# Cross-entropy of 256 rows on one core: the last partial sums in PSUM and added one by one, and new sizes for the loads

## The chip, the cores and the metric

The kernel runs on one core of a Trainium2 chip. The metric is the device time of one execution in microseconds; the median of several executions is compared.

## The reference

The inputs are logits (256 x 32000, fp32) and one label for each row. The result is one loss per row:

```python
log_probs = logits - np.max(logits, axis=-1, keepdims=True)
log_probs = log_probs - np.log(np.sum(np.exp(log_probs), axis=-1, keepdims=True))
return np.array([-log_probs[i, labels[i]] for i in range(batch)]).astype(np.float32)
```

That is the logarithm of the sum of exp(x) over a row, less the logit at the label. The kernel leaves out the maximum: it takes exp of the logits as they are, and multiplies the sum by exp(-logit at the label) before the logarithm.

## The kernel before, in words

The 256 rows are laid out as 128 partitions with two rows each, so a partition holds 64000 columns: row 0's 32000 and then row 1's. These columns are cut into 14 loads (`CHUNKS`), numbered 0 to 13, which SyncE's queue issues in order (`load`, L112). Loads 0 to 5 have buffers of their own. Load 6 takes over the buffer of load 2, and loads 7 to 13 lie side by side in `x_tail`, which takes over the buffer of load 1; so load 6 is issued once the exp of load 2 is done. The loads get smaller towards the end, so that little work is left when the last one lands.

ScalarE makes one pass over each load: `exps(i)` (L124) computes exp in place and sums along the columns into one accumulator, a column of `parts0` for row 0 or `parts1` for row 1. Load 3 holds the border between the two rows, so it is done in two pieces. On the chip each such call is two instructions, an ACTIVATE over the columns and an ACTIVATION_READ_ACCUMULATOR that writes the sum. The accumulator of the last load goes to a tile of its own, `s_last`.

Meanwhile GpSimd builds an identity matrix and gathers the logits at the labels (`g`); ScalarE takes exp(-g) (`eg`, L163), and VectorE multiplies the identity by it (`diag`, L165). A row is finished in this way: VectorE adds the columns of `parts` (`sums`), TensorE multiplies `sums` by `diag`, which gives the 128 scaled sums side by side on one partition of PSUM (`lane`), and ScalarE takes the logarithm (`log_row`, L132). Row 0 is finished in the middle of the stream (L169, L170). Row 1 is finished at the end: the reduction L177 waits for the accumulators up to load 12, L178 opens an accumulation in `lane1`, L180 adds `s_last` to it, then come the logarithm and the store of the result (L182).

After the exp of load 8 (`WARM_FROM`), TensorE is given 12 matmuls into a tile `warm` whose result nobody reads (L176). Every fp32 matmul is two instructions on TensorE, and each has a weight load.

The order on every engine is the order in which the program is written (`tc.manual_schedule()`); each engine works its queue from the front, and waits there for what its next instruction needs.

Of the kernel before, what the change touches and what calls it, by code (L numbers as in the profile page):

```python
# [9 lines left out]
P = 128  # L10
ROWS = 2
F32 = mybir.dt.float32
# [3 lines left out]


CHUNKS = [
    1024, 15104, 12672, 8960, 7136, 4992, 3872,
    2848, 2144, 1600, 1216, 992, 800, 640,  # L20
]
SLOTS = [0, 1, 2, 3, 4, 5, 2]
TAIL = len(SLOTS)
# [1 line left out]

WARM_FROM = 8
WARM = 12


def begin_first_load_before_barrier(nc):  # L30
# [15 lines left out]
@with_exitstack  # L46
def kernel(
    ctx: ExitStack,
    tc: tile.TileContext,
    logits: bass.AP,  # L50
    labels: bass.AP,
    out: bass.AP,
):
    nc = tc.nc
    nc.at_finalize(begin_first_load_before_barrier)
    B, C = logits.shape
    assert B == P * ROWS and sum(CHUNKS) == ROWS * C


    flat = logits.rearrange("(p r) c -> p (r c)", r=ROWS)  # L60


    pieces = []
    starts = []
    at = 0
    for n in CHUNKS:
        starts.append(at)
        cuts = [at] + [c for c in range(C, ROWS * C, C) if at < c < at + n] + [at + n]
        pieces.append([(a, b, a // C) for a, b in zip(cuts, cuts[1:])])
        at += n  # L70
    last = len(CHUNKS) - 1

    turn = next(i for i in range(len(CHUNKS)) if starts[i] + CHUNKS[i] >= C)

    big = ctx.enter_context(tc.tile_pool(name="big", bufs=1))
    small = ctx.enter_context(tc.tile_pool(name="small", bufs=1))
    psum = ctx.enter_context(tc.tile_pool(name="psum", bufs=1, space=bass.MemoryType.PSUM))

    width = {}
    for i, s in enumerate(SLOTS):  # L80
        width[s] = max(width.get(s, 0), CHUNKS[i])
    tiles = []
    for i, s in enumerate(SLOTS):
        tiles.append((big.tile([P, width[s]], F32, name=f"x{i}", tag=f"slot{s}"), starts[i]))
    tail = big.tile([P, width[TAIL_SLOT]], F32, name="x_tail", tag=f"slot{TAIL_SLOT}")
    assert sum(CHUNKS[TAIL:]) <= width[TAIL_SLOT]
    tiles += [(tail, starts[TAIL])] * (len(CHUNKS) - TAIL)

    n_of = [sum(1 for ps in pieces[:-1] for q in ps if q[2] == r) for r in range(ROWS)]
    parts = [small.tile([P, n_of[r]], F32, name=f"parts{r}") for r in range(ROWS)]  # L90
    s_last = small.tile([P, 1], F32, name="s_last")
    res = small.tile([1, ROWS * P], F32, name="res")
    sums = small.tile([P, ROWS], F32, name="sums")
    ident = small.tile([P, P], F32, name="ident")
    diag = [small.tile([P, P], F32, name=f"diag{r}") for r in range(ROWS)]
    lane = [psum.tile([1, P], F32, name=f"lane{r}") for r in range(ROWS)]
    warm = psum.tile([1, P], F32, name="warm")
    lbl = small.tile([P, 2 * ROWS], I32, name="lbl")
    idx = small.tile([P, ROWS], I32, name="idx")
    g = small.tile([P, ROWS], F32, name="g")  # L100
    eg = small.tile([P, ROWS], F32, name="eg")

    nc.scalar.preload_act_table_set("natural_log_exp_and_others")  # L103

    lbl_words = dataclasses.replace(
        labels.tensor, shape=[labels.tensor.shape[0] * 2], dtype=I32
    )

    def load(i):
        t, base = tiles[i]  # L110
        a, b = starts[i], starts[i] + CHUNKS[i]
        nc.sync.dma_start(out=t[:, a - base:b - base], in_=flat[:, a:b])  # L112

    seen = [0] * ROWS

    def exps(i):
        t, base = tiles[i]
        for a, b, r in pieces[i]:
            if i == last:
                acc = s_last[:, :]  # L120
            else:
                acc = parts[r][:, seen[r]:seen[r] + 1]
                seen[r] += 1
            nc.scalar.activation(  # L124
                out=t[:, a - base:b - base],
                in_=t[:, a - base:b - base],
                func=AF.Exp,
                accum_out=acc,
            )

    def log_row(r):
        nc.scalar.activation(  # L132
            out=res[0:1, r:ROWS * P:ROWS], in_=lane[r][:, :], func=AF.Ln
        )

    with tc.manual_schedule():
        first = len(set(SLOTS))
        for i in range(first):
            load(i)

        nc.scalar.dma_start(
            out=lbl[:, :], in_=bass.AP(tensor=lbl_words, offset=0, ap=[[2 * ROWS, P], [1, 2 * ROWS]])
        )
        nc.gpsimd.iota(out=idx[:, :], pattern=[[C, ROWS]], base=0, channel_multiplier=ROWS * C)
        make_identity(nc, ident[:, :])
        nc.gpsimd.tensor_add(out=idx[:, :], in0=idx[:, :], in1=lbl[:, 0:2 * ROWS:2])  # L146
        for r in range(ROWS):
            nc.gpsimd.indirect_dma_start(  # L148
                out=g[:, r:r + 1],
                out_offset=None,  # L150
                in_=logits[:, :],
                in_offset=bass.IndirectOffsetOnAxis(ap=idx[:, r:r + 1], axis=1),
            )


        done = 0
        for i in range(first, len(CHUNKS)):
            slot = SLOTS[i] if i < TAIL else TAIL_SLOT
            while done <= SLOTS[:first].index(slot):
                exps(done)  # L160
                done += 1
            load(i)
        nc.scalar.activation(out=eg[:, :], in_=g[:, :], func=AF.Exp, scale=-1.0)  # L163
        for r in range(ROWS):
            nc.vector.tensor_scalar_mul(diag[r][:, :], ident[:, :], eg[:, r:r + 1])  # L165
        for i in range(done, last):
            exps(i)
            if i == turn:
                nc.vector.reduce_sum(out=sums[:, 0:1], in_=parts[0][:, :], axis=mybir.AxisListType.X)  # L169
                nc.tensor.matmul(lane[0][:, :], sums[:, 0:1], diag[0][:, :], start=True, stop=True)  # L170
            if i == turn + 1:
                log_row(0)
            if i == WARM_FROM:
                col = parts[1][:, seen[1] - 1:seen[1]]
                for _ in range(WARM):
                    nc.tensor.matmul(warm[:, :], col, diag[0][:, :], start=True, stop=True)  # L176
        nc.vector.reduce_sum(out=sums[:, 1:2], in_=parts[1][:, :], axis=mybir.AxisListType.X)  # L177
        nc.tensor.matmul(lane[1][:, :], sums[:, 1:2], diag[1][:, :], start=True, stop=False)  # L178
        exps(last)
        nc.tensor.matmul(lane[1][:, :], s_last[:, :], diag[1][:, :], start=False, stop=True)  # L180
        log_row(1)
        nc.sync.dma_start(  # L182
            out=out.rearrange("(a n) -> a n", a=2), in_=res[0:1, :].rearrange("o (a n) -> o a n", a=2)
        )
# [30 lines left out]
```

The softmax here doesn't subtract the row's maximum and nothing guards it: scores larger than these inputs give would overflow.

## Time and profile before

| | |
|---|---|
| median of 5 runs | 84.49 us (84.3 to 86.21) |
| profiled execution, time | 85.67 us |
| profiled execution, span | 83.9 us |
| busy in the span: ScalarE | 58.4 us (70%) |
| busy: TensorE, matmul | 6.5 us (8%) |
| busy: VectorE | 0.8 us (1%) |
| logits read | 32.77 MB, mean 391 GB/s |
| DMA on the chain that ended last | 44% of the span |
| ScalarE on the chain that ended last | 32% of the span |

The slices of the page divide the span into 40 parts of 2.1 us, and a digit gives the busy tenths of a part. The chain of waits goes back from the last instruction to what released it at each step. In the timeline a line gives the start, the length, the engine and line, the operation, what it writes and reads, and in brackets the idle time ahead of it with what ended it. PE is TensorE's matmul, PEld its weight loads, ACT is ScalarE, DVE is VectorE.

### The profile page before, as it was taken

To read this page: it belongs to the slowest core of one execution; us is meant where nothing else is said; L and a number is where in the kernel's file an instruction comes from. 1 tells how busy PE (TensorE), PEld (TensorE's weight loads), DVE (VectorE), ACT (ScalarE), POOL (GpSimd) and SP (SyncE) were. 2 spreads that over 40 slices of the span, in tenths; PEclk is the share of its full clock that TensorE was granted. 3 is DMA by queue.
4 is the path that set the end of the run, shared out by engine and by line. 5 is a ranking of instruction groups with operands and counts; after the bars stand their busy time and mean duration, and the time that the engine had idled before them with its cause. 6 is when DMAs were issued, how large, how long until landed. Compare 5 with 4: busy or idle time off the path is not lost.

```text
span 83.9 us, 174 instructions
## 1 busy us (share of the span) xinstructions
PE 6.5 (8%) x30; PEld 3.4 (4%) x30; DVE 0.8 (1%) x4; ACT 58.4 (70%) x34; POOL 3.0 (4%) x10
## 2 busy tenths in 40 slices
PE   0000000000000000000000002000000000009980
PEld 0000000000000000000000000000000000005540
DVE  0000000000000000000000020000000000000000
ACT  6320000000299999909999999998999999999960
POOL 3000000000072000000000000000000000000000
PEclk9999999999999999999999999999999999999999
DMA  4999999998999989899997999999989999999200
GB/s 113 598 432 461 461 461 432 403 432 362 435 435 435 387 387 411 387 496 461 393 479 342 439 422 436 436 427 438 430 379 451 420 413 421 412 412 408 82 0 0
DMA packets 2226, 32.77 MB, mean 391 GB/s; under 512 B 433, under 2 KB 434, under 8 KB 1202
## 3 DMA queue, kind: packets, MB, share of 16 engines
q1 hardware_dynamic: 2018, 32.77, 92.0%
q10 hardware_dynamic: 144, 0.00, 0.1%
q0 software_dynamic: 64, 0.00, 0.1%
HBM read 32.77 MB, written 0.00 MB: 391 GB/s over the span
## 4 chain that ended last, share of the span: by engine, by line
DMA 44%; ACT 32%; issue 13%; PE 7%; SPq 0%; another core or an unknown queue 0%
DMA x<-in_logits_dram 44%; ACT x L124 26%; PE warm L176 6%; ACT x_tail L124 5%; ACT res L132 1%; PE lane L178 1%; SPq L112 0%; PE lane L180 0%; ACT eg L163 0%
## 5 line engine op out<-in xcount | busy, mean ns | idle before, releaser
L124 ACT ACTIVATE x<-x 128x1024 f32<-128x1024 f32 (+7 forms) x8 | 46.4, 5794 | 22.0 <-DMA x<-in_logits_dram 22.0
L124 ACT ACTIVATE x_tail<-x_tail 128x2848 f32<-128x2848 f32 (+6 forms) x7 | 9.8, 1404 | 0.0
L176 PE MATMUL warm<-diag,parts 128*1 128x128 f32 x24 | 5.3, 416 | 23.2 <-ACT x_tail L124 23.2
L170 PE MATMUL lane<-diag,sums 128*1 128x128 f32 x2 | 0.6, 397 | 51.8 <-DVE sums L169 51.8
L176 PEld LDWEIGHTS warm<-diag,parts 128*1 128x1 f32 x24 | 2.9, 122 | 25.6 <-ACT x_tail L124 23.7
L170 PEld LDWEIGHTS lane<-diag,sums 128*1 128x1 f32 x2 | 0.1, 80 | 51.8 <-DVE sums L169 51.8
L148 POOL DMA_INDIRECT g<-in_logits_dram,idx x2 | 2.1, 1040 | 0.6 <-issue 0.3
L103 ACT ACT_TABLE_LOAD x1 | 1.3, 1283 | 0.8 <-PEq L199 0.8
L124 ACT ACTIVATION_READ_ACCUMULATOR x<-x 128x1 f32 x8 | 1.5, 186 | 0.0
L124 ACT ACTIVATION_READ_ACCUMULATOR x_tail<-x_tail 128x1 f32 x7 | 1.3, 185 | 0.0
L132 ACT ACTIVATE res<-lane 1x128 f32<-1x128 f32 x2 | 0.5, 265 | 0.7 <-PE lane L180 0.7
L146 POOL TENSOR_TENSOR idx<-idx,lbl 128x2 int32<-128x2 int32 x1 | 0.2, 197 | 21.3 <-DMA lbl<-in_labels_dram 21.3
L165 DVE TENSOR_SCALAR diag<-ident,eg 128x128 f32<-128x128 f32 x2 | 0.5, 284 | 48.9 <-ACT eg L163 48.9
L178 PE MATMUL lane<-diag,sums 128*1 128x128 f32 x2 | 0.6, 418 | 0.0
L180 PE MATMUL lane<-diag,s_last 128*1 128x128 f32 x2 | 0.4, 302 | 0.0
L177 DVE TENSOR_REDUCE sums<-parts 128x1 f32<-128x10 f32 x1 | 0.2, 164 | 28.4 <-ACT x_tail L124 28.4
masks.py:199 POOL TENSOR_SCALAR_AFFINE_SELECT ident<-ident 128x128 f32<-128x128 f32 x1 | 0.3, 294 | 0.1
L178 PEld LDWEIGHTS lane<-diag,sums 128*1 128x1 f32 x2 | 0.3, 126 | 0.2
L180 PEld LDWEIGHTS lane<-diag,s_last 128*1 128x1 f32 x2 | 0.2, 122 | 0.2
masks.py:197 POOL MEMSET ident<- 128x128 f32 x1 | 0.2, 194 | 0.0
L163 ACT ACTIVATE eg<-g 128x2 f32<-128x2 f32 x1 | 0.2, 187 | 0.0
L169 DVE TENSOR_REDUCE sums<-parts 128x1 f32<-128x4 f32 x1 | 0.2, 157 | 2.3 <-ACT x L124 2.3
(5 smaller groups left out, 0.6 us busy)
## 6 DMA issues: line engine op xcount, KB each, us to landing
x<-in_logits_dram SPq DMA_DIRECT2D x1, 7552.0 KB, 21.8
x<-in_logits_dram SPq DMA_DIRECT2D x1, 6336.0 KB, 36.6
x<-in_logits_dram SPq DMA_DIRECT2D x1, 4480.0 KB, 46.7
x<-in_logits_dram SPq DMA_DIRECT2D x1, 3568.0 KB, 54.7
x<-in_logits_dram SPq DMA_DIRECT2D x1, 2496.0 KB, 60.0
x<-in_logits_dram SPq DMA_DIRECT2D x1, 1936.0 KB
x_tail<-in_logits_dram SPq DMA_DIRECT2D x1, 1424.0 KB, 21.6
x_tail<-in_logits_dram SPq DMA_DIRECT2D x1, 1072.0 KB, 23.7
```

Of the source, the lines that this page charges most:

```text
L103: nc.scalar.preload_act_table_set("natural_log_exp_and_others")
L124: nc.scalar.activation(out=t[:, a - base:b - base], in_=t[:, a - base:b - base], func=AF.Exp, accum_out=acc,)
L132: nc.scalar.activation(out=res[0:1, r:ROWS * P:ROWS], in_=lane[r][:, :], func=AF.Ln)
L146: nc.gpsimd.tensor_add(out=idx[:, :], in0=idx[:, :], in1=lbl[:, 0:2 * ROWS:2])
L148: nc.gpsimd.indirect_dma_start(out=g[:, r:r + 1], out_offset=None, in_=logits[:, :], in_offset=bass.IndirectOffsetOnAxis(ap=idx[:, r:r + 1 ...
L163: nc.scalar.activation(out=eg[:, :], in_=g[:, :], func=AF.Exp, scale=-1.0)
L165: nc.vector.tensor_scalar_mul(diag[r][:, :], ident[:, :], eg[:, r:r + 1])
L169: nc.vector.reduce_sum(out=sums[:, 0:1], in_=parts[0][:, :], axis=mybir.AxisListType.X)
L170: nc.tensor.matmul(lane[0][:, :], sums[:, 0:1], diag[0][:, :], start=True, stop=True)
L176: nc.tensor.matmul(warm[:, :], col, diag[0][:, :], start=True, stop=True)
L178: nc.tensor.matmul(lane[1][:, :], sums[:, 1:2], diag[1][:, :], start=True, stop=False)
L180: nc.tensor.matmul(lane[1][:, :], s_last[:, :], diag[1][:, :], start=False, stop=True)
```

## The change

The sizes of the 14 loads are new; their number, their order and their sum stay. Load 1 grows from 15104 to 16384 columns, and most of the last ones shrink.

The accumulators of loads 7 to 12 no longer go to columns of `parts1`. Each has a PSUM tile of its own (`far`). After the exp of such a load, VectorE copies the tile to SBUF (`near`), and TensorE multiplies it by `diag1` and adds it to `lane1`. The reduction of `parts1` and the matmul that opens the accumulation in `lane1` move from the end to just after the exp of load 6. At the end only `s_last` is left to be added. Both lanes now lie in one PSUM tile. The 12 warm matmuls stay behind load 8, now also behind the addition of load 8, and read a column of the exp's output instead of the accumulator.

So TensorE's queue from load 6 on is: the opening matmul, additions 7 and 8, the 12 warm matmuls, additions 9 to 12, and `s_last`. Before it was: the 12 warm matmuls, the opening matmul, and `s_last`.

```diff
 CHUNKS = [
-    1024, 15104, 12672, 8960, 7136, 4992, 3872,
-    2848, 2144, 1600, 1216, 992, 800, 640,
+    1024, 16384, 12512, 9024, 6656, 5088, 3744,
+    2688, 2016, 1504, 1120, 864, 736, 640,
 ]
...
+IN_PSUM = range(7, 13)
...
+    far = {i: psum.tile([P, 1], F32, name=f"far{i}") for i in IN_PSUM}
+    near = {i: small.tile([P, 1], F32, name=f"near{i}") for i in IN_PSUM}
...
-    lane = [psum.tile([1, P], F32, name=f"lane{r}") for r in range(ROWS)]
+    lane_tile = psum.tile([1, ROWS * P], F32, name="lane")
+    lane = [lane_tile[:, r * P:(r + 1) * P] for r in range(ROWS)]
...
+            elif i in IN_PSUM:
+                acc = far[i][:, :]
...
+            if i == IN_PSUM[0] - 1:
+                nc.vector.reduce_sum(out=sums[:, 1:2], in_=parts[1][:, :], axis=mybir.AxisListType.X)
+                nc.tensor.matmul(lane[1][:, :], sums[:, 1:2], diag[1][:, :], start=True, stop=False)
+            if i in IN_PSUM:
+                nc.vector.tensor_copy(out=near[i][:, :], in_=far[i][:, :])
+                nc.tensor.matmul(lane[1][:, :], near[i][:, :], diag[1][:, :], start=False, stop=False)
             if i == WARM_FROM:
-                col = parts[1][:, seen[1] - 1:seen[1]]
+                at = starts[i] - tiles[i][1]
+                col = tiles[i][0][:, at:at + 1]
                 for _ in range(WARM):
                     nc.tensor.matmul(warm[:, :], col, diag[0][:, :], start=True, stop=True)
-        nc.vector.reduce_sum(out=sums[:, 1:2], in_=parts[1][:, :], axis=mybir.AxisListType.X)
-        nc.tensor.matmul(lane[1][:, :], sums[:, 1:2], diag[1][:, :], start=True, stop=False)
         exps(last)
         nc.tensor.matmul(lane[1][:, :], s_last[:, :], diag[1][:, :], start=False, stop=True)
         log_row(1)
```

More of the change, by code (lines that the diff above doesn't have):

```diff
@@ L87 @@
     tiles += [(tail, starts[TAIL])] * (len(CHUNKS) - TAIL)
-    n_of = [sum(1 for ps in pieces[:-1] for q in ps if q[2] == r) for r in range(ROWS)]
+    n_of = [
+        sum(1 for ps in pieces[:IN_PSUM[0]] for q in ps if q[2] == r) for r in range(ROWS)
+    ]
+    assert all(len(pieces[i]) == 1 for i in IN_PSUM) and turn < IN_PSUM[0]
+    far = {i: psum.tile([P, 1], F32, name=f"far{i}") for i in IN_PSUM}
+    near = {i: small.tile([P, 1], F32, name=f"near{i}") for i in IN_PSUM}
     parts = [small.tile([P, n_of[r]], F32, name=f"parts{r}") for r in range(ROWS)]
```

## The prediction

> **What bounds the kernel now.** I read the slices of the page first, then the chain of waits, then the last ten microseconds instruction by instruction.
>
> ```profile
> PE   0000000000000000000000002000000000009980
> ACT  6320000000299999909999999998999999999960
> DMA  4999999998999989899997999999989999999200
> ```
>
> The DMA row is full up to slice 37; ScalarE (ACT) is full from slice 12, with dips where it waits for a load. The logits come in at a fixed pace and the exps follow them closely. PE works only in the last four slices, almost without a gap.
>
> ```profile
> 75.55 0.04 issue
> 75.59 5.28 PE warm L176 x24
> 80.87 0.43 PE lane L178 x2
> 81.30 0.25 PE lane L180 x2
> 81.54 0.02 issue
> 81.57 0.27 ACT res L132
> ```
>
> These are the last pieces of the chain of waits: start, length, what. The end already comes through TensorE's queue: 24 warm passes (each fp32 matmul is two instructions, a pass each), L178's two, L180's two, then the logarithm. The timeline of the same stretch shows how little room TensorE has:
>
> ```profile
> 75.35 0.18 ACT L124 ACTIVATION_READ_ACCUMULATOR x_tail<-x_tail 128x1 f32 x1
> ...
> 75.59 5.28 PE L176 MATMUL warm<-diag,parts 128*1 128x128 f32 x24 [23.16 <-ACT x_tail L124]
> ...
> 79.93 0.18 ACT L124 ACTIVATION_READ_ACCUMULATOR x_tail<-x_tail 128x1 f32 x1
> 80.03 0.72 ACT L124 ACTIVATE x_tail<-x_tail 128x640 f32<-128x640 f32 x1
> 80.15 0.16 DVE L177 TENSOR_REDUCE sums<-parts 128x1 f32<-128x10 f32 x1 [28.36 <-ACT x_tail L124]
> 80.45 0.34 PEld L178 LDWEIGHTS lane<-diag,sums 128*1 128x1 f32 x2
> 80.65 0.18 ACT L124 ACTIVATION_READ_ACCUMULATOR x_tail<-x_tail 128x1 f32 x1
> 80.66 0.63 PE L178 MATMUL lane<-diag,sums 128*1 128x128 f32 x2
> 80.89 0.33 PEld L180 LDWEIGHTS lane<-diag,s_last 128*1 128x1 f32 x2
> 81.09 0.44 PE L180 MATMUL lane<-diag,s_last 128*1 128x128 f32 x2
> 81.57 0.27 ACT L132 ACTIVATE res<-lane 1x128 f32<-1x128 f32 x1 [0.73 <-PE lane L180]
> ```
>
> The warm passes start when load 8's accumulator is read and run for 5.28 us; ScalarE's remaining work from there also takes 5.3 us (75.45 to 80.74). The two meet at the end by a hair: s_last was ready at 80.83, its weights loaded at 80.89, and its first pass started at 81.09, 0.21 behind L178's second (80.88). TensorE is a second limit of equal height beside ScalarE. That decides what follows.
>
> How long is one pass? From the first warm pass (75.59) to L178's first (80.66) lie 24 passes: 0.211 us each. The answers for L176 and L180 add their durations:
>
> ```profile
> L176 PE MATMUL warm<-diag,parts x24: 371/418/418, 75.6 to 80.5; 128*1 128x128 f32 x24
> ```
>
> ```profile
> L180 PE MATMUL lane<-diag,s_last x2: 273/302/331, 81.1 to 81.3; 128*1 128x128 f32 x2
> ```
>
> The same shape takes 418 ns up to 80.9, 331 at 81.09 and 273 at 81.26: TensorE got faster only at about 81.1, some 5.5 us after the chain of passes began, although the page's PEclk prints 9 in every slice. So the warm passes run slow, and only the very last ones fast. The length of a fast pass is bounded by these rows: if of the 418 ns only the 211 of the pitch shrinks, 273 leaves 0.066 us; if all shrinks alike, 0.211 x 273/418 = 0.138. I take the middle, 0.105.
>
> **The change, part by part.** The profiled execution took 85.67 us for a span of 83.9, so 1.77 lies outside. It is 1.18 above the median of the runs, 84.49; I work out a difference on this execution and carry it to the median.
>
> *Sizes.* The total is the same, so the last load lands when it did: by the trace's completions at 79.68. Between completions I interpolate by columns (1.19 ns per column from load 1 on, nearly straight). The new loads 1 to 6 land at 24.1, 39.1, 49.8, 57.7, 63.7 and 68.1 (before: 22.6, 37.8, 48.4, 56.8, 62.7, 67.3). An exp costs 0.833 ns per column ((2558 - 719) / (2848 - 640)) and 0.19 per piece (load 8's 2144 columns: 73.47 to 75.45). Walking ScalarE along these, it ends at 80.73 for the old sizes (the trace: 80.74) and 80.68 for the new. The later arrival of load 1 is hidden by a smaller stall before load 2 (1.1 for 2.3). Sizes alone: -0.05. They also move the end of load 8's exp, which releases TensorE: the loads 0 to 8 hold 384 columns more, and it ends 0.2 to 0.3 later.
>
> *Accumulators in PSUM.* From one READ_ACCUMULATOR to the next exp pass 0.10 us (75.35 to 75.45). No row writes one to PSUM. The nearest with a PSUM operand is L132: 63.00 to the next exp at 63.16, less 128 x 0.833 ns, leaves 0.05, where eg, two columns from SBUF, leaves 0.09 (48.56 to 48.65). I take 0.04 less for each of six, -0.25 in all, because that row has the same engine and the memory in question; the ends are 0 (the saving belongs to reading only) and -0.09 x 6 = -0.55, with +0.25 as its mirror. The walk then ends at 80.43, -0.30, load 8's accumulator at 75.62 (before 75.44), and ScalarE starts each of the last seven loads within 0.1 of its landing where it now is 0.2 to 0.35 behind.
>
> [...]
>
> *Copies on VectorE.* Six copies of 128x1, each waiting for one accumulator. VectorE is otherwise idle here, so they cost nothing to ScalarE; what they cost is on TensorE's path. Start about 0.11 after the accumulator, as L177 did (80.03 to 80.15); length between L177's 0.16 and L165's 0.28, I take 0.2; 0.05 to TensorE (L169 to L170). The addition of load 8 thus reaches TensorE at about 76.0. Row 1's early sum (L184, L185 of the new file) and the addition of load 7 run in gaps before that and cost nothing; if they were late they would only push this start.
>
> *Additions on TensorE.* This is where the price lies. The queue runs in order: addition 8 (2 passes), warm (24), additions 9 to 12 (8), s_last (2). Twelve warm matmuls still stand in front of four additions whose data come at 77 to 80, and in front of s_last. From 75.59 there were 28 passes; now there are 36 from 76.0, as addition 8 with its detour over VectorE stands ahead of the warm ones too, which only wait for ScalarE. L178 no longer comes behind them, which is in that count.
>
> With the slow pass throughout, the last of 36 starts at 76.0 + 35 x 0.211 = 83.4 and ends at 83.8, against 81.53: +2.3. If TensorE turns fast as long after the chain's start as before (5.5: at 81.5), 26 passes are begun by then, the 36th starts at 82.4 and ends, with 273 ns, at 82.7: +1.2. If it turns fast at the same moment as before (81.1), 24 are begun, and it ends at 82.5: +1.0. If it turned 2 us sooner than before, at 79.1, 15 are begun, the 36th starts at 81.3 and ends at 81.5: no difference. All of this is later than ScalarE needs (s_last at about 80.6, end then near 81.2), so the 0.30 gained there is not seen.
>
> [...]
>
> Of +1.0 and +1.2 I take +1.0, the unchanged moment, because a little more work (row 1's sum, addition 7) now precedes the chain. For the profiled execution that is 86.7, for the median 84.49 + 1.0 = 85.5.
>
> **Rivals.**
>
> 1. *ScalarE sets the end* (faster). TensorE would have to make its 35 steps by 80.9, within 4.9 us of 76.0; with 0.211 and 0.105 that means at most 12 slow ones, so fast passes from 78.5 on, 2.6 us sooner than in the trace. Then the whole -0.30 comes through, 84.2; from 79.1 back, a part of it. For it: the trace holds only one such turn, and does not show what sets its moment. Against: that one came after 5.5 us of unbroken passes, and here it would need half.
>
> 2. *No difference.* The turn comes close to 79.1, and the overhang of TensorE eats just what ScalarE gains: 84.3 to 84.7. It needs two sizes to meet.
>
> 3. *Slow to the end.* Fast passes are seen for two instructions only, and nothing in the trace says that they must come by 83.4. Without them +2.0 to +2.3, some 86.6.
>
> 4. *The change doesn't do what it says:* a saved accumulator read of 0. Then load 8 ends at 75.70 instead of 75.62, and the forecast moves by +0.1 only, since TensorE ends last; it is in the forecast's range.
>
> **How the numbers follow.** Forecast (TensorE ends last, turning fast within 1.5 us of 81.1 either way, which by the same count gives +0.2 to +1.7): 0.68. Slow to the end: 0.13. ScalarE sets the end: 0.13. No difference: 0.06. The range, 84.5 to 86.5, takes the forecast with its unknown moment and most of the slow case, and leaves out the faster one and the slowest runs, together under 0.2. About 0.2% (0.17 us) is what a measurement of this kernel can tell from no change. Faster 0.13, same 0.06, slower 0.81.
>
> **What would show it.** Right: in the profile after, the last exp ends up to 0.3 earlier against the last landing, the passes of additions 9 to 12 follow the warm ones without a gap although their copies were done before, and the idle time of the last L132 before "PE lane" grows from 0.73 to about 2. READ_ACCUMULATOR of a PSUM tile to the next exp takes 0.06 rather than 0.10. Wrong: if TensorE idles ahead of s_last, or its passes are near 0.105 apart before 79, rival 1 holds; if ScalarE stalls in the tail, the sizes were mis-walked.

## The result, and the profile after

The changed kernel is slower, by about half of what was forecast. Over 52 runs of it and 94 of the kernel before, the ratio is 1.0054 (95% interval 1.0031 to 1.0076), about +0.46 us; the medians of all runs are 85.82 and 85.21 us. On one chip side by side (the run `a_again` below) it is 1.0069 (1.0031 to 1.0107), +0.58 us, and the medians of all runs are 85.39 and 84.44. A ratio leaves out every run over 1.5% above the fastest of its kernel, here 27 of the 52 and 35 of the 94, whatever made them long, so executions in which TensorE turned fast late may be among them and +0.46 may be too small. The forecast was +1.0, that is 85.5, with a range of 84.5 to 86.5.

The profiled execution took 84.67 us for a span of 82.9. These are the last pieces of its chain of waits (start, length, what):

```profile
74.90 0.17 DVE near L187
75.07 0.04 issue
75.11 0.59 PE lane L188 x2
75.70 3.73 PE warm L193 x24
79.43 0.87 PE lane L188 x8
80.31 0.23 PE lane L195 x2
80.54 0.02 issue
80.56 0.27 ACT res L142
```

From addition 8 to the logarithm, the chain is TensorE alone: addition 8, the warm passes, additions 9 to 12 (x8), s_last. ScalarE's tail, five exps long, is not on it. The timeline of the same stretch tells when each part was ready:

```profile
74.71 0.16 ACT L134 ACTIVATION_READ_ACCUMULATOR x_tail<-x_tail 128x1 f32 x1
74.76 1.45 ACT L134 ACTIVATE x_tail<-x_tail 128x1504 f32<-128x1504 f32 x1
74.90 0.16 DVE L187 COPY near<-far 128x1 f32<-128x1 f32 x1 [1.67 <-ACT x_tail L134]
...
75.11 0.59 PE L188 MATMUL lane<-diag,near 128*1 128x128 f32 x2 [1.25 <-DVE near L187]
...
76.31 0.16 DVE L187 COPY near<-far 128x1 f32<-128x1 f32 x1 [1.25 <-ACT x_tail L134]
...
79.27 1.04 PE L188 MATMUL lane<-diag,near 128*1 128x128 f32 x8
79.48 0.23 ACT L134 ACTIVATION_READ_ACCUMULATOR x_tail<-x_tail 128x1 f32 x1
80.04 0.19 PEld L195 LDWEIGHTS lane<-diag,s_last 128*1 128x1 f32 x2
80.14 0.38 PE L195 MATMUL lane<-diag,s_last 128*1 128x128 f32 x2
80.56 0.27 ACT L142 ACTIVATE res<-lane 1x128 f32<-1x128 f32 x1 [0.85 <-PE lane L195]
```

Load 9's copy was done at 76.47, and its addition waited until 79.27 behind the warm matmuls. s_last was ready at 79.71 and its first pass began at 80.14. The accumulator now costs 0.05 us to the next exp (74.71 to 74.76), where it was 0.10. And the warm passes are not what they were in the first profile of before:

```profile
L193 PE MATMUL warm<-diag,x_tail x24: 272/276/417, 75.5 to 79.2; 128*1 128x128 f32 x24
```

Their median is 276 ns where it was 418: TensorE turned fast at 77.85, in the middle of the warm matmuls and 2.7 us after addition 8 began, not 5 after it. So this execution lost little: its logarithm starts only 0.85 after the last accumulator.

### The profile page after: what moved, and what is told of

Read it like the earlier page. It is cut to its first block, busy times and chain, and to the rows that moved or that the text cites. A ratio compares the mean times of both kernels' runs of the same rounds, so it can differ in the third digit from the quotient of the medians.

```text
span 82.9 us, 204 instructions
## 1 busy us (share of the span) xinstructions
PE 7.2 (9%) x42; PEld 3.7 (4%) x42; DVE 1.7 (2%) x10; ACT 58.2 (70%) x34; POOL 3.0 (4%) x10
## 4 chain that ended last, share of the span: by engine, by line
DMA 45%; ACT 32%; issue 13%; PE 7%; SPq 0%; DVE 0%
DMA x<-in_logits_dram 45%; ACT x L134 26%; ACT x_tail L134 5%; PE warm L193 5%; PE lane L188 2%; ACT res L142 1%; SPq L120 0%; PE lane L195 0%; DVE near L187 0%; ACT eg L173 0%
## 5 line engine op out<-in xcount | busy, mean ns | idle before, releaser
L134 ACT ACTIVATE x<-x 128x1024 f32<-128x1024 f32 (+7 forms) x8 | 46.9, 5866 | 21.0 <-DMA x<-in_logits_dram 21.0
L134 ACT ACTIVATE x_tail<-x_tail 128x2688 f32<-128x2688 f32 (+6 forms) x7 | 9.1, 1346 | 0.0
L193 PE MATMUL warm<-diag,x_tail 128*1 128x128 f32 x24 | 3.9, 338 | 0.0
L193 PEld LDWEIGHTS warm<-diag,x_tail 128*1 128x1 f32 x24 | 2.5, 105 | 1.4
L188 PE MATMUL lane<-diag,near 128*1 128x128 f32 x12 | 2.2, 313 | 3.1 <-DVE near L187 3.1
L187 DVE COPY near<-far 128x1 f32<-128x1 f32 x6 | 0.9, 158 | 7.4 <-ACT x_tail L134 7.4
L188 PEld LDWEIGHTS lane<-diag,near 128*1 128x1 f32 x12 | 0.8, 83 | 4.3 <-DVE near L187 4.1
L195 PE MATMUL lane<-diag,s_last 128*1 128x128 f32 x2 | 0.4, 272 | 0.0
```

Source lines behind the costliest of these rows:

```text
L134: nc.scalar.activation(out=t[:, a - base:b - base], in_=t[:, a - base:b - base], func=AF.Exp, accum_out=acc,)
L187: nc.vector.tensor_copy(out=near[i][:, :], in_=far[i][:, :])
L188: nc.tensor.matmul(lane[1][:, :], near[i][:, :], diag[1][:, :], start=False, stop=False)
```

## The experiments

Two theories and a third stood against each other. Queue: TensorE is still busy with the warm matmuls and four additions when s_last is ready. Sizes (or their landings): ScalarE or the DMA queues lose. Clock: the last passes are slow, wherever they stand. For each kernel the table gives the ratio to before on the same chip (for the changed one's first profile, over all its runs), and, from its profile, two stretches of the end: from the last landing (by the trace's completions) to the end of the last accumulator, which is ScalarE's part, and from there to the start of the last logarithm, which is TensorE's. The last column, the turn, is how long after the start of unbroken passes TensorE turned fast, by the clock's record in the trace, or by the lengths of the passes where it has none.

| kernel | ratio (95%) | ScalarE's part | TensorE's part | turn |
|---|---|---|---|---|
| before, first profile | | 1.16 | 0.73 | 5.6 |
| b_again | | 1.10 | 0.47 | 3.8 |
| changed, first profile | 1.0054 (1.0031 to 1.0076) | 0.98 | 0.85 | 2.7 |
| a_again | 1.0069 (1.0031 to 1.0107) | 0.97 | 1.77 | 4.6 |
| e1_sizes_only | 1.0035 (1.0004 to 1.0065) | 1.20 | 0.47 | 3.7 |
| e2_old_sizes | 1.0103 (1.0068 to 1.0138) | 0.89 | 1.48 | 4.7 |
| e3_warm0 | 1.0004 (0.9979 to 1.0028) | 0.98 | 0.68 | none |
| e3_warm6 | 0.9987 (0.9959 to 1.0016) | 0.98 | 0.72 | none before the end |
| e3_warm18 | 1.0304 (1.0264 to 1.0343) | 0.98 | 2.30 | 3.0 |
| e6_same12_moved | 0.9978 (0.9955 to 1.0002) | 0.99 | 0.47 | 2.7 |
| e2_old_sizes_warm6 | 0.9980 (0.9955 to 1.0004) | 0.89 | 0.47 | 3.8 |
| e4_old_sizes_early | 0.9968 (0.9951 to 0.9985) | 0.88 | 0.47 | 4.3 |
| e5_one_reduction_old | 1.0082 (1.0054 to 1.0109) | 1.85 | 0.47 | 5.2 |
| e7_one_reduction_early | 1.0083 (1.0056 to 1.0111) | 1.83 | 0.47 | 4.4, behind a pause |

The end of b_again shows what before has when TensorE turns fast early enough: it waits for ScalarE (0.44), and the logarithm follows the last accumulator by 0.47.

```profile
79.74 0.18 ACT L124 ACTIVATION_READ_ACCUMULATOR x_tail<-x_tail 128x1 f32 x1
79.97 0.09 PEld L180 LDWEIGHTS lane<-diag,s_last 128*1 128x1 f32 x2 [0.44 <-ACT x_tail L124]
79.97 0.38 PE L180 MATMUL lane<-diag,s_last 128*1 128x128 f32 x2
80.39 0.27 ACT L132 ACTIVATE res<-lane 1x128 f32<-1x128 f32 x1 [0.47 <-PE lane L180]
```

**The warm matmuls in the changed kernel: none, 6, 18.** A number is changed:

```diff
-WARM = 12
+WARM = 0
```

> The changed kernel without any of the 12 warm matmuls. Queue theory: each addition is done when its copy arrives, s_last finds TensorE free, and only the slow last passes are paid: -0.5 us against the changed kernel, -0.1 to 0 against before. Clock theory (the loss is that the last passes come at the slow clock, not that they queue): all passes are slow now, so it is slower than the changed kernel by 0.2 us or more. Size theory: as the changed kernel, +0.4 against before.

> The changed kernel with 6 warm matmuls in place of 12. Queue theory: addition 8 and the 6 are 14 passes, 3.0 us at 0.211, so they end near 78.1, the additions 9 to 12 catch up just before the last accumulator, and the end follows s_last within about 0.7 us: -0.1 to -0.3 us against before. Size theory: as the changed kernel, +0.4 against before. Clock theory: fewer warm passes, so later fast passes: not faster than the changed kernel.

> The changed kernel with 18 warm matmuls in place of 12: 12 more passes ahead of the additions. Queue theory: they add 12 x 0.109 = 1.3 us where they run fast and up to 12 x 0.211 = 2.5 where slow; about +1.4 us against the changed kernel, +1.8 against before. Size theory: no change against the changed kernel, since nobody reads warm. Clock theory: the last passes are fast more often, so not slower than the changed kernel.

Measured: 84.54, 84.32 and 86.97 us, where before had 84.47 beside them. The timeline of the kernel with none:

```profile
79.27 0.59 PE L188 MATMUL lane<-diag,near 128*1 128x128 f32 x2 [0.18 <-DVE near L187]
79.51 0.23 ACT L134 ACTIVATION_READ_ACCUMULATOR x_tail<-x_tail 128x1 f32 x1
79.79 0.09 PEld L195 LDWEIGHTS lane<-diag,s_last 128*1 128x1 f32 x2 [0.43 <-ACT x_tail L134]
79.79 0.59 PE L195 MATMUL lane<-diag,s_last 128*1 128x128 f32 x2
80.41 0.27 ACT L142 ACTIVATE res<-lane 1x128 f32<-1x128 f32 x1 [0.68 <-PE lane L195]
```

Here TensorE waits for ScalarE (0.43 before L195), not the other way. The two passes of s_last are slow (0.59 together, 0.38 when fast), and still the kernel is half a microsecond quicker than the changed one. The clock theory falls: without any fast pass it should have been the slower. With 18 the end moves by another 2.1 us by the ratios, or 1.6 against the changed kernel's 85.39 on another chip, where 1.4 was expected and 1.3 to 2.5 the bounds. The profiled run, the shortest of the six, turned fast at 78.14, ahead of the added passes; that the longer ones turned later, and had some of them slow, is likely and not shown. The sizes are the same in all three, so they are not what makes the three differ. With 6 the direction was right, but the gain against before, expected at -0.1 to -0.3, is -0.1 and not clear of zero. All its passes were slow, too (s_last's two 0.63 together).

**The same 12, at other places.**

```diff
-WARM_FROM = 8
-WARM = 12
+WARM_AFTER = {6: 6, 7: 3, 8: 3}
...
-            if i == WARM_FROM:
+            if i in WARM_AFTER:
...
-                for _ in range(WARM):
+                for _ in range(WARM_AFTER[i]):
```

> The changed kernel with the same 12 warm matmuls, 6 placed after load 6, 3 after load 7 and 3 after load 8: nothing is added or left out, only the place in TensorE's queue is another. Queue theory: the 6 run from 71 to 73.5, the next 3 end near 75.6, the last near 77.3, each addition comes on time: -0.15 to -0.3 us against before. If the loss is the number of TensorE instructions, the copies or the sizes: as the changed kernel.

> The changed kernel again, beside the others on one chip. Queue theory with an unsteady turn of TensorE's clock (seen from 2.7 to 5.8 us after unbroken passes begin): its end moves by half of what the turn moves, so +0.5 to +0.9 us against before on the same chip, and its runs spread by up to 1.5 us where those of the kernel before spread by 0.6. If the turn is always early, as in its first profile (2.7): +0.1 to +0.2.

84.28 us against 84.44 of before and 85.39 of the changed kernel beside it; the gain against before, 0.9978 (0.9955 to 1.0002), is not quite clear of zero. Every instruction of the changed kernel is there, and what separates the two, 0.8 us by the ratios and 1.1 between the medians, is only their order on TensorE, with the earlier turn (73.84) that comes of it. This is the cleanest of the runs. Its timeline, at the end:

```profile
75.53 0.82 PE L192 MATMUL warm<-diag,x_tail 128*1 128x128 f32 x6
76.71 0.38 PE L187 MATMUL lane<-diag,near 128*1 128x128 f32 x2 [0.37 <-DVE near L186]
...
79.44 0.38 PE L187 MATMUL lane<-diag,near 128*1 128x128 f32 x2 [0.38 <-DVE near L186]
79.68 0.23 ACT L133 ACTIVATION_READ_ACCUMULATOR x_tail<-x_tail 128x1 f32 x1
79.96 0.38 PE L194 MATMUL lane<-diag,s_last 128*1 128x128 f32 x2
80.37 0.27 ACT L141 ACTIVATE res<-lane 1x128 f32<-1x128 f32 x1 [0.47 <-PE lane L194]
```

Each addition waits for its copy (0.37, 0.38), and the logarithm starts 0.47 after the last accumulator.

The changed kernel's second profile shows the other end of its spread. Its chain and its warm passes:

```profile
74.95 0.58 PE lane L188 x2
75.54 4.66 PE warm L193 x24
80.19 0.87 PE lane L188 x8
81.07 0.23 PE lane L195 x2
81.30 0.02 issue
81.32 0.27 ACT res L142
```

```profile
L193 PE MATMUL warm<-diag,x_tail x24: 272/417/417, 75.3 to 79.9; 128*1 128x128 f32 x24
```

The turn came 4.6 us after addition 8 began, 1.9 later than in the first, and from addition 8 to the logarithm there are 6.37 us instead of 5.45 (81.32 - 74.95, 80.56 - 75.11): 0.92 more, about half of 1.9, which fits the measured step from one pass to the next, 0.213 us before the turn and 0.109 after it. This execution took 85.46 us, the first 84.67, with the same work. The 12 runs lie from 84.61 to 86.33, those of before beside them from 84.27 to 85.23.

**The sizes.** One kernel is before with the new `CHUNKS`, another the changed one with the old.

> The kernel before with only the 14 new sizes. Queue theory (the changed kernel ends late because TensorE still works through the warm matmuls and four additions when s_last is ready): the sizes cost nothing, -0.1 to +0.1 us against before, and TensorE's last matmul comes as soon after the last accumulator as before. Size theory (the larger load 1 and the new landings delay ScalarE or the DMA queues): it shows the whole loss, +0.4 us or more.

> The kernel before, for a second profile. Walk theory (the first profile's loads landed late; in most executions they land sooner, and ScalarE then has no stall after load 2, so larger loads 1 and 2 only delay its start): the last landing is near 78.8 as with the new sizes, load 2 lands 1 to 1.4 us before the new load 2's 38.2, ScalarE idles nowhere after it or by under 0.1, and its last accumulator is done near 79.8, 0.3 before the sizes-only kernel's 80.09. DMA theory (the 65536-byte rows of the new load 1 move worse): the last landing is 0.3 earlier than the new sizes' 78.8.

> The changed kernel with the sizes of before. Walk theory: -0.3 us against the changed kernel, so +0.1 to +0.2 against before, all of it TensorE's queue. If the sizes matter only in the kernel without PSUM accumulators: as the changed kernel, +0.45.

> The changed kernel with the sizes of before and 6 warm matmuls. Walk theory with the queue theory: both losses are out and the cheaper accumulators are left, -0.3 to -0.45 us against before (ratio 0.995 to 0.9965). If the sizes are no loss here: as the 6-warm kernel with the new sizes, -0.1.

The sizes alone: 1.0035 (1.0004 to 1.0065), +0.30 us, so not nothing, where -0.1 to +0.1 was expected, and below the whole loss. The expectation for b_again fell in its main point: before does stall after load 2, by 0.29 ahead of load 4, also where the loads land early, and the last landing is 78.82 against 78.89, so the DMA side loses nothing either.

```profile
55.94 6.15 ACT L124 ACTIVATE x<-x 128x7136 f32<-128x7136 f32 x1 [0.29 <-DMA x<-in_logits_dram]
```

What the profiles agree on is ScalarE's part: 1.10 to 1.20 without PSUM, 0.88 to 0.99 with a PSUM tile for each accumulator. The new sizes cost ScalarE 0.10 us in both. Load 2 landed at 38.0 to 38.3 with the new sizes (seven profiles) and at 36.7 to 36.9 with the old (six, without the first), and the new ones leave no later stall that could absorb it. In time this 0.1 was not separated: with 6 warm matmuls the two sizes give 0.9987 and 0.9980, where the old ones were expected at 0.995 to 0.9965, and with 12 the old ones look no better (1.0103, where 0.3 us less than the changed kernel was expected). That profile had a turn at 4.7 and TensorE's part at 1.48, so a tenth on ScalarE does not show there; its interval overlaps that of a_again, so neither size is shown to be quicker. Why the sizes alone cost 0.30 in time and 0.10 on ScalarE is not shown. One way is through TensorE: with the new sizes its warm matmuls begin 0.49 later (75.16 against 74.67 in b_again) and the last accumulator is done only 0.17 later (80.09 against 79.92), so a late turn would cost more; its one profile did not catch one.

**Warm matmuls early, old sizes.**

```diff
...
-WARM_FROM = 8
-WARM = 12
+WARM_AFTER = {6: 8, 8: 8}
...
```

> As the last, but with 8 warm matmuls after load 6 and 8 after load 8, so TensorE is busy from about 71 on. Queue theory with the clock's turn seen 2.7 to 5.8 us after unbroken passes begin: the turn comes by 77, the additions do not pile up, s_last's two passes run fast (0.38 instead of 0.6 us): -0.5 to -0.6 us against before. If the turn comes no earlier than with the other kernels (78 to 81), the 16 matmuls pile up like the 18 did: +0.5 or more.

84.28 us against 84.56 of before: 0.9968 (0.9951 to 0.9985), the only kernel clearly quicker than before, by 0.27 us where -0.5 to -0.6 was expected. By the profiles the gain is ScalarE's 0.22; TensorE's part is 0.47, and that is what before already has when its turn comes early. It also removes the spread: 11 of its 12 runs lie within 0.21 us.

**PSUM accumulators without the additions.** This is the kernel before, with the accumulators of row 1 up to load 12 in one PSUM tile, which the old reduction reads; the warm matmuls read a column of the exp's output. The second kernel has its warm matmuls at other places, too.

```diff
-    parts = [small.tile([P, n_of[r]], F32, name=f"parts{r}") for r in range(ROWS)]
+    parts = [(small, psum)[r].tile([P, n_of[r]], F32, name=f"parts{r}") for r in range(ROWS)]
...
```

> The kernel before, with all accumulators of row 1 up to load 12 in one PSUM tile that the old reduction reads; sizes, warm matmuls and TensorE's queue as before. PSUM theory (0.05 us less per read accumulator, 0.28 in all at the last one): -0.2 to -0.3 us against before, a little less where TensorE's warm matmuls end last. If the saving comes only with separate tiles (the reduction and ScalarE meet in one PSUM tile): 0 or slower.

> As the last, with 8 warm matmuls after load 6 and 10 after load 8 in place of 12 after load 8. Queue theory: the clock turns by 77, the warm matmuls end before 78.5 in any case, s_last's passes run fast and TensorE adds nothing: -0.35 to -0.5 us against before, and the runs spread less than those of the last kernel.

Both are slower by 0.8% where a gain was expected. The first one's timeline shows where the time goes:

```profile
74.88 0.15 ACT L124 ACTIVATION_READ_ACCUMULATOR x_tail<-x_tail 128x1 f32 x1
75.07 1.54 ACT L124 ACTIVATE x_tail<-x_tail 128x1600 f32<-128x1600 f32 x1
...
76.51 0.15 ACT L124 ACTIVATION_READ_ACCUMULATOR x_tail<-x_tail 128x1 f32 x1
76.70 1.22 ACT L124 ACTIVATE x_tail<-x_tail 128x1216 f32<-128x1216 f32 x1
```

From the accumulator to the next exp 0.19 us pass, where separate tiles have 0.05 and one SBUF tile 0.10. The same profile has 0.05 where the next sum goes to another tile: from the accumulator of load 12, the last in the PSUM tile, to the exp of load 13, whose sum goes to `s_last` (79.90 to 79.95). So the longer gap comes with the shared PSUM tile; what makes it is not shown. ScalarE's part grows to 1.85. So the many tiles, with the copies and additions that they bring, are not decoration: the separate tiles are what makes the 0.05 possible here. The second kernel, with more warm matmuls, could not mend that; its turn came at 79.3 where 77 was expected.

## Why the prediction was right or wrong

**Right: the mechanism and the sign.** Additions 9 to 12 follow the warm passes without a gap although their copies were long done, and s_last waits behind them. With the order alone changed the loss is gone. No profile of the changed kernel has ScalarE's end last, as rival 1 would.

**Right, by measured rows.** PSUM accumulators: from the start of load 8's exp to that of load 13's, five pieces, it takes 5.92 us (72.94 to 78.86), and 6.12 with SBUF (73.15 to 79.27 in e1_sizes_only), so 0.04 less per piece, as forecast, and ScalarE's part is 0.22 shorter at either sizes, for -0.25. Copies: 0.16 for 0.2, and addition 8 begins 0.35 after load 8's exp gives way (74.76 to 75.11), for 0.38. A fast pass: 0.109 us (eight additions from 79.27 to s_last at 80.14), for 0.105.

**Mis-sized: the moment at which TensorE turns fast.** The sum took it 5.1 us after addition 8 begins (81.1 against 76.0), because the one profile of before had it that late. In the profiles that show it, it came between 2.7 and 5.6 us after unbroken passes began. The forecast's own count of TensorE's length holds at both ends: with its 0.211 and 0.105 us it gives about 5.4 us from addition 8 to the logarithm for a turn after 2.7, and 6.3 for one after 4.6; the two profiles show 5.45 and 6.37. Against b_again, whose logarithm starts at 80.39, they are 0.17 (80.56) and 0.93 (81.32) later, and the timed difference, 0.46 to 0.58, lies between. The extreme taken for the typical hit twice, in opposite directions: it made the changed kernel's TensorE too late, and in that first profile before itself had lost 0.26 (0.73 against 0.47) of TensorE's time, which made the difference too small. That the second error took back part of the first is luck.

**Wrong by a little: the sizes.** -0.05 was forecast, ScalarE's part grew by 0.10 instead. Interpolated between the old landings, the new load 2 comes 1.33 later; it came about 1.4 later, and no stall after it takes that in. The rest of the 0.15 is not explained, nor is the larger loss in time (+0.30).

The forecast's width, 1.5 us either way around 81.1, or 3.6 to 6.6 after addition 8, was the author's estimate, and no run shows it: the two profiles of the changed kernel turned 2.7 and 4.6 after, so the moment differs from run to run. The earliest turns came 2.7 after unbroken passes began, in two profiles, and 3.0 in one. The step from one pass to the next about halves there, from 0.213 us to 0.109. And ScalarE's shorter way to the next exp, taken from a row that reads PSUM, holds for a written accumulator (0.05 for 0.10).

Rival 3, slow to the end, was not seen in a profile of the changed kernel.

## What to carry to other kernels

Filler work stands in the same queue as the work that it is meant to help: when real work is added at the end of that queue, move the filler ahead of it or shorten it (here 0.9978 and 0.9987 of before, where the changed kernel has 1.0069). If one profile shows an event that can fall at another moment in the next execution, as the turn did here (2.7 and 4.6 us in two profiles of one kernel), take a second profile before its moment goes into a sum. Here an accumulator in PSUM was cheaper for ScalarE only where each had a tile of its own (0.05 us to the next exp, 0.19 in a shared tile, 0.10 in SBUF).

## What the runs showed of the hardware that was not expected

The turn to fast passes is not a matter of the number of passes alone: in e6_same12_moved it came after 13 passes (71.09 to 73.84), while in e7_one_reduction_early 16 passes ran from 70.13 to 73.7, paused for 1.18 us, and the 20 that followed were all slow up to 78.89. In e4_old_sizes_early, where additions and warm matmuls follow each other without that pause, the turn came at 74.6. That the pause is the cause was not tested.

The last piece behind PSUM accumulators gives back part of the saving: from the start of load 13's exp to the end of its accumulator it takes 0.85 us (78.86 to 79.71) and 0.82 with the others in SBUF (79.27 to 80.09 in e1_sizes_only), although its own accumulator lies in SBUF in both. So the 0.25 of six times 0.04 comes to 0.22 or a little less. The exps of the changed kernel are also recorded up to 0.04 longer, 0.84 for 0.80 at 736 columns, but that costs no time: the read of the accumulator begins 0.71 after the exp in both (78.10 to 78.81, 78.47 to 79.18).
